# Late modulation rows summed on VectorE by half parts, partition sum by products with ones

## The chip, the cores and the metric

The kernel runs on one core of a Trainium2 chip. The metric is the device time of one execution in microseconds (us). Engines are called by the names of the profile: PE is TensorE (PEld its weight loads), DVE is VectorE, ACT is ScalarE, POOL is GpSimd, SP is SyncE, which here only issues DMAs.

## The reference, cut to what matters

One layer of a hybrid block over 1024 latent tokens and 256 context tokens, width 1024, all in fp32. The part that is changed is the modulation vector of the latent stream:

```python
mod = jax.nn.silu(c) @ w_ada[i] + b_ada[i]            # (1, 6 * 1024)
sh1, sc1, g1, sh2, sc2, g2 = jnp.split(mod[:, None, :], N_MOD, axis=-1)
...
h = modulate(rmsnorm(x, norm1_g[i]), sh1, sc1)
q, k, v, hv, hx1, hx2, gna, ghy = jnp.split(h @ w_in[i], IN_SPLITS, axis=-1)
...
x = x + g1 * gated_merge(gna, ghy, y_na, y_hy, w_na_o[i], w_hy_o[i], w_out[i])
h2 = modulate(rmsnorm(x, norm2_g[i]), sh2, sc2)
x = x + g2 * swiglu(h2, ffn_w1[i], ffn_w3[i], ffn_w2[i])
```

The parts sh1 and sc1 are needed at once. The other four (g1, sh2, sc2, g2: parts 2 to 5 of 1024 columns each) are needed only after the two mixers. For them the kernel must form, for each of 4096 columns, a sum over 1024 rows of `w_ada` times silu(c), 16 MB of weights in all.

## The kernel before, in words

The kernel runs in stages: first the early modulation and the normed, transposed input (`hidden`); then the input projection of 40 chunks of 128 columns (`project`, line 574), beside which the long convolution is done; then the attention; the gated merge; and the feed-forward part.

The projection multiplies in three products of split operands. `weights` (line 178) loads a chunk's 512 KB into the raw tile `wr` (one buffer) from SP's queue, ACT rounds it into `wh` and DVE subtracts to make `wl` (`split`, line 173), and `gemm` (line 187) issues 24 matmuls of 128x512 for each half of the tokens.

Beside it runs a generator called `side` (line 963). It first makes the spectra of the convolution's filters (`filters`, line 348, with `forward` and `dft`) merged with the late modulation rows (`ada_rows`, line 872), and then the convolutions (`conv`, line 449). `_merged` takes the next step of the generator that is least advanced by the amounts that the steps yield: 97 for the filters against 39 for `ada_rows`, and SIDE = 496 for `side` against 39 for the projection. This sets the order in which the program is written down; the framework then puts the instructions of each engine into an order of its own by readiness and by this order, and sets all waits. Each engine executes its list strictly in that order, and so does SP with the DMAs that it issues.

A filter step loads two tiles `dec` of 256 KB (two buffers), makes two products into `filt_ps` on PE and multiplies them with `dec` on DVE into `fv` (line 370). After four steps DVE does a run of sums (`fx`, `fv`, `x`, `b`, `a`: lines 378 to 430), and PE transforms the tiles `a` (`dft_ps`, lines 442 to 444) with matrices `matf`. ACT copies the results out and SP stores them (`spec`, line 390). All the products of this side work take their PSUM bank from one pool of five (`psf`).

`ada_rows` goes over two pairs of parts, (3, 4) and (2, 5). For a pair it takes a tile `arow` of 128x512, zeroes it and loads the bias into four of its rows (POOL). For each part and each k of 8 it loads 128 rows of `w_ada` over 1024 columns, 512 KB, into the ring `wal` of three, and issues four products of 256 columns, one into each group of 32 columns of the PE array (`tile_position`), with silu(c) in column 0 of the 32-column weights `cs` (line 889). They are added up in one PSUM tile `ar_ps` that is held for the whole pair. At the end one DVE addition (line 893) joins it to the bias, POOL stores the rows to DRAM, and for the first pair PE transposes them into `mod2`. Each of the 32 steps yields 1.2.

Of the kernel before, what the change touches and what calls it, by code (L numbers as in the profile page):

```python
# [10 lines left out]
F32 = mybir.dt.float32  # L11
F32R = mybir.dt.float32r
AF = mybir.ActivationFunctionType
ALU = mybir.AluOpType
# [4 lines left out]
P = 128  # L19
D = 1024  # L20
# [138 lines left out]
class Block:  # L159
# [712 lines left out]
    def ada_rows(self, pool, psf):  # L872


        nc, a = self.nc, self.a
        for pair in ((3, 4), (2, 5)):
            r = pool.tile([P, 512], F32, tag="arow", name="arow", bufs=1)
            nc.gpsimd.memset(r, 0.0)
            for n, part in enumerate(pair):
                for j in range(4):  # L880
                    at = part * D + 256 * j
                    nc.gpsimd.dma_start(r[32 * j:32 * j + 1, 256 * n:256 * n + 256], a["b_ada"][0:1, at:at + 256])
            ps = psf.tile([P, 512], F32, tag="f", name="ar_ps")
            for n, part in enumerate(pair):
                for k in range(8):
                    w = pool.tile([P, D], F32, tag="wal", name="wal", bufs=3)
                    nc.sync.dma_start(w, a["w_ada"][k, :, part * D:(part + 1) * D])
                    for j in range(4):
                        nc.tensor.matmul(ps[32 * j:32 * j + 32, 256 * n:256 * n + 256], self.cs[:, 2 * k:2 * k + 32],
                                         w[:, 256 * j:256 * j + 256], start=(k == 0), stop=(k == 7),  # L890
                                         tile_position=(0, 32 * j))
                    yield 1.2
            nc.vector.tensor_add(r, ps, r)
            for n, part in enumerate(pair):
                for j in range(4):
                    nc.gpsimd.dma_start(self.modd[part][0:1, 256 * j:256 * j + 256],
                                        r[32 * j:32 * j + 1, 256 * n:256 * n + 256])
            if pair[0] == 3:
                pt = psf.tile([P, 512], F32, tag="f", name="ada_t")
                for j in range(4):  # L900
                    nc.tensor.transpose(pt[:, j * P:(j + 1) * P], r[:, j * P:(j + 1) * P], self.ident)
                v = pt.rearrange("p (n h g q) -> p n q g h", n=2, h=2, g=4)[:, :, 0]
                cols = lambda t: t.rearrange("p (g h) -> p g h", h=2)
                nc.vector.tensor_copy(cols(self.mod2[:, 1, :]), v[:, 0])
                nc.vector.scalar_tensor_tensor(cols(self.mod2[:, 0, :]), v[:, 1], 1.0, cols(self.ng[:, 1, :]),
                                               op0=ALU.add, op1=ALU.mult)
# [207 lines left out]
    def sums(self, wa, psf, xs, raw, h2):  # L1114

        nc = self.nc
        for k in range(4):
            b = []
            for kk in (k, k + 4):
                pt = psf.tile([P, 512], F32, tag="f", name="hT_ps")  # L1120
                for j in range(4):
                    mm = nc.tensor.transpose(pt[:, j * P:(j + 1) * P], xs[j][:, kk * P:(kk + 1) * P], self.ident)
                    if j == 0:
                        self.tc.keep_in_program_order(mm)
                h = wa.tile([P, 512], F32, tag="t", name="htmp")
                nc.scalar.activation(h, pt, AF.Identity, bias=self.mod2[:, 1, kk:kk + 1],
                                     scale=self.mod2[:, 0, kk:kk + 1])
                b.append(h)
            put = lambda n, src: self.split(h2[n][0][:, k, :], h2[n][1][:, k, :], src)
            b12, b22 = b  # L1130
            b11, b21 = raw[:, k, :], raw[:, k + 4, :]
            nc.vector.tensor_sub(b11, b12, b11)
            put(5, b11)
            nc.vector.tensor_sub(b12, b22, b12)
            put(7, b12)
            nc.vector.tensor_sub(b11, b22, b11)
            put(6, b11)
            put(3, b22)
            nc.vector.tensor_sub(b21, b21, b11)
            put(4, b21)  # L1140
            yield
# [312 lines left out]
```

## Time and profile before

| | us |
|---|---|
| median of three runs | 1719.76 (1718.63 to 1722.28) |
| the profiled execution | 1721.66 |
| its span in the trace | 1719.9 |
| PE busy | 1669.8, 97% of the span |
| DVE busy | 1187.3, 69% |
| ACT busy | 662.2, 39% |

The busy time of an engine is the time in which at least one of its instructions runs; matmuls overlap in the pipeline, so that the sum of their durations is larger. An fp32 matmul appears as two instructions in the trace, so `x8` is four products. Durations are those of one profiled execution. A release ("<-") names what ended an idle time. In rows by stretch stand the stretch, its length, the busy time of PE, PEld, DVE, ACT and POOL (with their instructions), the granted PE clock as a share of full speed, the busy share of the DMA engines, and GB/s.

### The profile page before, as it was taken

To read this page: it belongs to the slowest core of one execution; us is meant where nothing else is said; L and a number is where in the kernel's file an instruction comes from. 1 tells how busy PE (TensorE), PEld (TensorE's weight loads), DVE (VectorE), ACT (ScalarE), POOL (GpSimd) and SP (SyncE) were. 2 spreads that over 40 slices of the span, in tenths; PEclk is the share of its full clock that TensorE was granted. 3 is DMA by queue.
4 is the path that set the end of the run, shared out by engine and by line. 5 is a ranking of instruction groups with operands and counts; after the bars stand their busy time and mean duration, and the time that the engine had idled before them with its cause. 6 is when DMAs were issued, how large, how long until landed. Compare 5 with 4: busy or idle time off the path is not lost.

```text
span 1719.9 us, 22909 instructions
## 1 busy us (share of the span) xinstructions
PE 1669.8 (97%) x8348; PEld 1311.0 (76%) x8348; DVE 1187.3 (69%) x2006; ACT 662.2 (39%) x1141; POOL 152.7 (9%) x273
## 2 busy tenths in 40 slices
PE   6999999999999999999999999999999999999997
PEld 2766766777777777888787788788888888878886
DVE  3665266699995966565865867867866566479566
ACT  4711222312221224455654325733333333355455
POOL 0100210101010004020200001010101001100000
PEclk9999999999999999999999999999999999999999
DMA  9375556645554456344657524333432323395344
GB/s 357 108 252 198 170 196 207 216 159 180 172 180 157 159 178 193 125 144 129 202 171 241 165 68 165 129 122 129 153 105 94 108 92 105 111 381 176 99 121 153
DMA packets 109910, 282.51 MB, mean 164 GB/s; under 512 B 15327, under 2 KB 24163, under 8 KB 107493
## 3 DMA queue, kind: packets, MB, share of 16 engines
q1 hardware_dynamic: 89864, 219.99, 38.2%
q0 software_dynamic: 19280, 60.60, 10.5%
q8 instruction: 66, 1.08, 0.3%
q10 hardware_dynamic: 653, 0.44, 0.1%
q14 instruction: 47, 0.39, 0.1%
HBM read 213.60 MB, written 67.39 MB: 163 GB/s over the span
## 4 chain that ended last, share of the span: by engine, by line
PE 44%; issue 26%; DVE 5%; DMA 5%; POOL 3%; ACT 1%; SPq 0%; POOLq 0%; ACTq 0%; DVEq 0%
PE in_ps L195 11%; PE out_ps L1091 5%; PE dx_ps L1322 5%; PE x_ps L1153 4%; PE dz_ps L1322 3%; PE dft_ps L442 2%; PE hy_ps L195 2%; PE pt_ps L800 2%; PE pt_ps L786 2%; PE na_ps L195 1%; POOL g L1266 1%; DMA ar<-g 1%; PE dft_ps L443 1%; PE dy_ps L1322 1%; PE dft_ps L444 1%
## 5 line engine op out<-in xcount | busy, mean ns | idle before, releaser
L195 PE MATMUL in_ps<-hTh,wl 128*128 128x512 f32 x640 | 259.3, 406 | 2.1 <-ACT proj L614 1.7
L195 PE MATMUL in_ps<-hTh,wh 128*128 128x512 f32 x640 | 253.2, 396 | 0.0
L195 PE MATMUL in_ps<-hTl,wh 128*128 128x512 f32 x640 | 252.6, 395 | 0.3 <-DVE hTl L176 0.2
L195 PEld LDWEIGHTS in_ps<-hTh,wl 128*128 128x128 f32 x640 | 120.7, 189 | 33.6 <-issue 5.1
L195 PEld LDWEIGHTS in_ps<-hTh,wh 128*128 128x128 f32 x640 | 120.8, 189 | 28.0 <-issue 1.6
L195 PEld LDWEIGHTS in_ps<-hTl,wh 128*128 128x128 f32 x640 | 120.9, 189 | 26.7 <-DVE hTl L176 1.9
L176 DVE TENSOR_TENSOR wl<-wr,wh 128x1024 fp32r<-128x1024 f32 (+1 forms) x56 | 59.8, 1068 | 95.7 <-ACT wh L175 95.6
L175 ACT CAST wh<-wr 128x1024 fp32r<-128x1024 f32 (+1 forms) x56 | 51.9, 926 | 135.6 <-PE in_ps L195 109.1
L176 DVE TENSOR_TENSOR ol<-ws,oh 128x512 fp32r<-128x512 f32 x88 | 60.4, 688 | 48.7 <-ACT oh L175 48.5
L176 DVE TENSOR_TENSOR ol<-ar,oh 128x512 fp32r<-128x512 f32 x77 | 52.8, 688 | 47.0 <-ACT oh L175 47.0
L175 ACT CAST oh<-ar 128x512 fp32r<-128x512 f32 x77 | 47.9, 622 | 83.6 <-PE dx_ps L1322 33.1
L175 ACT CAST oh<-ws 128x512 fp32r<-128x512 f32 x88 | 54.7, 622 | 57.5 <-PE x_ps L1153 27.4
L775 ACT ACTIVATE pe<-pe,mx 128x640 f32<-128x640 f32 x64 | 52.6, 823 | 49.3 <-DVE mx L774 49.3
L1322 PE MATMUL dx_ps<-ol,oh 128*128 128x512 f32 x176 | 68.7, 390 | 1.7 <-DVE ol L176 1.7
L442 PE MATMUL dft_ps<-a,matf 128*128 128x512 f32 x128 | 66.2, 598 | 4.0 <-DVE a L430 3.1
L1322 PE MATMUL dx_ps<-oh,ol 128*128 128x512 f32 x176 | 67.3, 390 | 2.0 <-DVE ol L176 2.0
L774 DVE CUSTOM_DVE_ANT_0 pe<-s_ps,bias 128x640 f32<-128x640 f32 x64 | 50.1, 820 | 27.7 <-PE s_ps L769 27.7
L1322 PE MATMUL dx_ps<-oh 128*128 128x512 f32 x176 | 68.5, 389 | 0.0
L175 ACT CAST oh<-wr 128x512 fp32r<-128x512 f32 x70 | 43.3, 622 | 51.5 <-PE x_ps L1153 16.0
L176 DVE TENSOR_TENSOR ol<-wr,oh 128x512 fp32r<-128x512 f32 x70 | 48.0, 688 | 21.2 <-ACT oh L175 21.0
L370 DVE TENSOR_TENSOR fv<-filt_ps,dec 128x512 f32<-128x512 f32 x32 | 21.5, 688 | 51.7 <-DMA dec<-in_decay 32.1
L1093 DVE TENSOR_TENSOR x<-x,out_ps 128x512 f32<-128x512 f32 x64 | 42.7, 684 | 19.1 <-PE out_ps L1091 18.9
(391 smaller groups left out, 4191.4 us busy)
## 6 DMA issues: line engine op xcount, KB each, us to landing
wr<-in_w SPq DMA_DIRECT2D x52, 512.0 KB, 3.6
wr<-in_w_in SPq DMA_DIRECT2D x40, 512.0 KB, 4.5
ar<-g SPq DMA_DIRECT2D x77, 256.0 KB, 2.8
wal<-in_w_ada SPq DMA_DIRECT2D x32, 512.0 KB, 6.6
matf<-in_dft_f SPq DMA_DIRECT2D x32, 384.0 KB, 4.4
bias<-in_rpb SPq DMA_DIRECT2D x64, 192.0 KB, 3.7
g<-t POOLq DMA_DIRECT2D x47, 256.0 KB, 3.0
w<-in_w SPq DMA_DIRECT2D x44, 256.0 KB, 5.4
```

What stands on the lines that cost most here:

```text
L175: self.nc.scalar.copy(hi, src)
L176: self.nc.vector.tensor_sub(lo, src, hi.bitcast(F32))
L195: mm = nc.tensor.matmul(ps, ww[:, k * P:(k + 1) * P], xx[:, k, pos:pos + width], start=(i == 0), stop=(i == n - 1))
L442: nc.tensor.matmul(ps, m[:, 0], v.rearrange("p a b -> p (a b)"), start=True, stop=False)
L774: nc.vector.tensor_tensor_reduce(pe, ps[:, 256:896], bt, -1.0, 3e38, ALU.add, ALU.min, mx[:, 0:1])
L775: nc.scalar.activation(pe, pe, AF.Exp, bias=mx[:, 0:1], scale=-1.0, accum_out=mx[:, 1:2])
L786: pin(nc.tensor.transpose(pt[:, at:at + P], pe[:, c * P:(c + 1) * P], self.ident))
L800: pin(nc.tensor.matmul(pt[ch, 1280:1408], vv[:, ch], pts[:, hh, c * P:(c + 1) * P], start=(c == 0), stop=(c == 4), tile_position=(0, 64 * ...
L1091: nc.tensor.matmul(ps, gg[x][:, tk], ww[y][:, sl], start=(i == 0), stop=(i == n - 1))
L1093: nc.vector.tensor_add(x1[:, sl], x1[:, sl], ps)
L1153: mm = nc.tensor.matmul(ps, w[u][:, k * P:(k + 1) * P], x[v][:, k, :], start=(start and k == 0 and i == 0), stop=(stop and k == 3 and i == 2),
L1322: nc.tensor.matmul(ps[j], x[u][:, j * P:(j + 1) * P], w[v], start=(start and i == 0 and c == 0), stop=(stop and i == N - 1 and k == len(re ...
```

## The change: what it does, and the diff

The products with `cs` go. Instead DVE sums over k: for each part of a pair and each half of 512 columns, eight loads of 128x512 (256 KB, ring `wal` of four, tag `wal2`) are multiplied with the column of silu(c) of their k, which is a scalar for each partition, and added into a tile `acc` (ring `aacc` of two); the first is a multiplication alone. When all eight are in, two products with a 128x32 tile of ones sum `acc` over its partitions, each over 256 columns and into a column group of its own (0 and 32 for the first half, 64 and 96 for the second), into a PSUM tile that is taken for that alone. A DVE addition of 64x256 joins it to the bias in `arow`. Each of the 64 steps yields 0.6. The bias loads, the stores and the transposition stay.

```diff
     def ada_rows(self, pool, psf):
         nc, a = self.nc, self.a
+        ones = pool.tile([P, 32], F32, name="ones", tag="ones", bufs=1)
+        nc.gpsimd.memset(ones, 1.0)
+
+        def sums(r, pair):
+            for n, part in enumerate(pair):
+                for h in range(2):
+                    acc = pool.tile([P, 512], F32, tag="aacc", name="aacc", bufs=2)
+                    for k in range(8):
+                        w = pool.tile([P, 512], F32, tag="wal2", name="wal", bufs=4)
+                        at = part * D + 512 * h
+                        nc.sync.dma_start(w, a["w_ada"][k, :, at:at + 512])
+                        c = self.cs[:, 2 * k:2 * k + 1]
+                        if k:
+                            nc.vector.scalar_tensor_tensor(acc, w, c, acc, op0=ALU.mult, op1=ALU.add)
+                        else:
+                            nc.vector.tensor_scalar(acc, w, c, None, op0=ALU.mult)
+                        yield 0.6
+                    ps = psf.tile([P, 512], F32, tag="f", name="ar_ps")
+                    for j in range(2):
+                        g = 64 * h + 32 * j
+                        nc.tensor.matmul(ps[g:g + 32, 0:256], ones, acc[:, 256 * j:256 * j + 256], start=True,
+                                         stop=True, tile_position=(0, g))
+                    rs = r[64 * h:64 * h + 64, 256 * n:256 * n + 256]
+                    nc.vector.tensor_add(rs, ps[64 * h:64 * h + 64, 0:256], rs)
+
         for pair in ((3, 4), (2, 5)):
...
-            ps = psf.tile([P, 512], F32, tag="f", name="ar_ps")
-            for n, part in enumerate(pair):
-                for k in range(8):
-                    w = pool.tile([P, D], F32, tag="wal", name="wal", bufs=3)
-                    nc.sync.dma_start(w, a["w_ada"][k, :, part * D:(part + 1) * D])
-                    for j in range(4):
-                        nc.tensor.matmul(ps[32 * j:32 * j + 32, 256 * n:256 * n + 256], self.cs[:, 2 * k:2 * k + 32],
-                                         w[:, 256 * j:256 * j + 256], start=(k == 0), stop=(k == 7),
-                                         tile_position=(0, 32 * j))
-                    yield 1.2
-            nc.vector.tensor_add(r, ps, r)
+            yield from sums(r, pair)
```

## Rows read from the trace of the kernel before

**Rows 1.** The page, part 1: engine busy us (share) x instructions.

```profile
span 1719.9 us, 22909 instructions
PE 1669.8 (97%) x8348; PEld 1311.0 (76%) x8348; DVE 1187.3 (69%) x2006; ACT 662.2 (39%) x1141; POOL 152.7 (9%) x273
```

**Rows 2.** Busy time by stage: the filters, then the convolutions.

```profile
77.00:322.00 245.00, 233.52 (x1267) 170.21 (x1267) 134.28 (x184) 52.36 (x86) 31.30 (x55) 0.98 0.61 204
322.00:640.00 318.00, 317.61 (x1337) 241.42 (x1335) 268.42 (x462) 73.88 (x107) 22.11 (x33) 1.00 0.51 173
```

**Rows 3.** The chain that ended last, in order of time: start, us, what.

```profile
287.25 11.16 PE in_ps L195 x48
...
306.84 0.43 PE dft_ps L443 x2
```

**Rows 4.** Busy time by stretch of the tile `ar_ps` alone: its last line, the sum.

```profile
sum 322.00, PE 18.78 PEld 6.29 DVE 1.37; mean PE 1.44 PEld 0.48 DVE 0.11
```

**Rows 5.** Timeline of PE around one step of `ada_rows`, and around three in a row.

```profile
97.09 0.40 PE L195 MATMUL in_ps<-hTh,wl 128*128 128x512 f32 x1
97.42 0.64 PE L889 MATMUL ar_ps<-wal,cs 128*32 128x256 f32 x8
97.98 0.50 PE L195 MATMUL in_ps<-hTl,wh 128*128 128x512 f32 x1
...
106.27 1.50 PE L889 MATMUL ar_ps<-wal,cs 128*32 128x256 f32 x24
```

**Rows 6.** Groups of DVE instructions by line and shape: busy us, mean ns | idle before.

```profile
L430 DVE SCALAR_TENSOR_TENSOR a<-x,b 128x512 f32<-128x512 f32 x64 | 42.2, 684 | 10.0 <-PE dft_ps L444 9.8
L425 DVE SCALAR_TENSOR_TENSOR x<-b 128x256 f32<-128x256 f32 x32 | 13.3, 417 | 0.0
L504 DVE TENSOR_SCALAR e<-e 128x512 f32<-128x512 f32 x8 | 3.3, 418 | 0.1
```

**Rows 7.** What PE waited for between 77 and 330 us: total, times, longest.

```profile
PE filt_ps L363 <- DVE fv L370: 2.9, 2, 2.4
PE ar_ps L889 <- DMA wal<-in_w_ada: 2.7, 3, 1.7
PE dft_ps L442 <- DVE a L430: 2.7, 1, 2.7
```

**Rows 8.** All waits between 77 and 320 us: two of DVE's.

```profile
DVE wl L176 <- ACT wh L175: 40.5, 8, 13.5
...
DVE fv L370 <- DMA dec<-in_decay: 32.1, 15, 6.8
```

**Rows 9.** What SP's queue waited for between 60 and 330 us.

```profile
SPq L181 <- DVE wl L176: 56.9, 11, 13.8
SPq L887 <- PE ar_ps L889: 49.0, 13, 11.7
```

**Rows 10.** Busy time by stretch around a PE stop, columns as in rows 2.

```profile
142.00:144.00 2.00, 0.25 (x1) 0.25 (x2) 0.69 (x1) 0.00 (x0) 0.00 (x0) 1.00 0.84 301
144.00:146.00 2.00, 1.50 (x7) 0.92 (x7) 0.69 (x1) 0.00 (x0) 0.00 (x0) 0.75 0.42 162
146.00:148.00 2.00, 2.00 (x7) 1.16 (x5) 0.69 (x1) 0.00 (x0) 0.00 (x0) 0.50 0.82 219
148.00:150.00 2.00, 2.00 (x6) 1.60 (x5) 0.69 (x1) 0.00 (x0) 0.00 (x0) 0.50 0.82 301
150.00:152.00 2.00, 2.00 (x6) 1.52 (x5) 0.69 (x1) 0.00 (x0) 0.00 (x0) 0.54 0.44 137
```

**Rows 11.** DMA issues: KB each, median us to landing.

```profile
wal<-in_w_ada SPq DMA_DIRECT2D x32, 512.0 KB, 6.6
...
dec<-in_decay SPq DMA_DIRECT2D x32, 256.0 KB, 3.9
```

**Rows 12.** Busy time by stretch inside the convolutions, columns as in rows 2.

```profile
408.00:500.00 92.00, 92.00 (x392) 69.69 (x391) 87.68 (x149) 22.79 (x32) 9.17 (x13) 1.00 0.52 175
500.00:600.00 100.00, 99.61 (x410) 75.30 (x409) 79.63 (x139) 20.16 (x29) 3.76 (x7) 1.00 0.47 160
```

## The prediction

> **What bounds the kernel now.** I read the page's engine shares first: PE is busy 97% of 1719.9 us, DVE 69% [rows 1]. Then the busy time by stage. `ada_rows` runs inside the filter stage, 77 to 322 us: there PE is busy 233.52 of 245 us and DVE only 134.28; in the convolutions behind it PE is busy 317.61 of 318 and DVE 268.42 [rows 2]. A busy PE need not be at its peak, so third comes the chain that ended last: within this stage it runs over PE, and 48 projection matmuls take 11.16 us [rows 3], 0.2325 us each. The chain shows no wait within them, and the granted clock of the stage is 0.98 of full speed [rows 2]: PE's list is the bound here, and work taken out of it is time, as long as the list stays filled. Last come the waits: PE's waits for DVE and for loads in this stage, three kinds, are 8.3 us in all [rows 7], while DVE's own idle time there is 245 − 134.28 = 110.7 us.
>
> So the question is whether work goes from the bound engine to one with room, and what the new coupling of the two costs.
>
> **The products that go.** All instructions on `ar_ps` keep PE busy 18.78 us [rows 4]. That this is time on the path, not overlap, shows in one step: the projection matmul before it starts at 97.09, the one behind it at 97.98, and without the step it would have followed after 0.2325 us; so a single step costs 0.66 us. Three steps in a row are busy 1.50 us, thus 0.43 for each further one, and 0.23 for going in and out [rows 5]. The 32 steps lie in 22 runs, counted in the timeline: 32 × 0.43 + 22 × 0.23 = 18.8 us, the same number. With them go PE's waits for the `wal` loads, 2.7 us [rows 7].
>
> **The products that come.** Eight sums (two pairs, two parts, two halves), each closed by two products of 256 columns. No row shows two column groups. One fp32 product of 256 columns over the full array takes 0.43 us (its two instructions) [rows 3], four in four column groups took the same 0.43 [rows 5]; a pair lies between these, so it is 0.43 plus 0.23 for going in and out: 8 × 0.66 = 5.3 us. Were the two groups done one after the other it would be 8 × 1.09 = 8.7 us. I take 5.3: the four groups did overlap. The Trainium skill, "TensorE: Matmul & The Clock Gate", section "Measured speedup vs the span model", puts the span of packed products at one product plus about 4 ns for each further tile; no run here shows it for two, and by it the pair would also stay at 0.66. Net for PE: −18.8 − 2.7 + 5.3 = −16.2 us.
>
> **DVE.** Per sum one multiplication, seven multiply-adds and one addition of 64x256. A multiply-add of 128x512 lasts 684 ns, a 128x512 multiplication by a scalar 418, an operation of 256 columns 417 [rows 6]. 8 × (7 × 0.684 + 0.418 + 0.417) = 45.0 us, less the two old additions of 0.69: +43.6. DVE's load in the stage goes to 134.3 + 43.6 = 178 us of some 229, 78%. That is room on average, so I cost the work itself at nothing: its cover is the 110.7 us of idle time, most of it DVE standing at `wl` for ACT's rounding (40.5 us) and at `fv` for `dec` (32.1) [rows 8]. But DVE keeps its order. A multiply-add written behind such a wait stands with it, and the runs that end in the tiles `a`, which PE needs, get longer by the multiply-adds mixed in. In return a multiply-add that stands for its load holds up `fv`, `wl` and `a` behind it, and PE waits for all three.
>
> **The new wait.** PE's pair of products waits for the eighth multiply-add, and the projection's matmuls stand behind it in PE's list. The old steps waited for a load alone, 2.7 us over 32. The nearest rows: PE's waits for DVE at `filt_ps` and `dft_ps` were 5.6 us over 64 groups of products, at most 2.66 us each [rows 7]. Bounds for eight pairs are thus 8 × 0.09 = 0.7 us and 8 × 2.66 = 21.3 us. Nothing below zero: a wait that is added gives nothing back. I take 0.5 us a pair, 4 us, nearer the lower end, since the framework places the pair by readiness and has projection matmuls to put before it, as with `dft_ps`; but the chain is longer (eight loads, eight dependent sums), and the real landing times vary.
>
> **Loads.** The bytes stay; 32 loads of 512 KB become 64 of 256 KB. The former landed after 6.6 us, `dec` loads of 256 KB on the same queue after 3.9 [rows 11], so a half costs less than a whole. The ring holds 1 MB ahead instead of 1.5. SP's order matters more: it stood 49.0 us because PE had not released a `wal` buffer, and `dec`, `matf`, `spec` and `wr` stood behind; 56.9 us it stood at `wr` [rows 9]. DVE will release the halves instead. I take zero here, with −2 (earlier `dec`) and +3 us (DVE in its long waits releases late) as bounds, about PE's whole wait for `fv` today [rows 7] to either side. 32 more issues are hidden by SP's idle time.
>
> **PSUM, POOL, clock.** `ar_ps` no longer holds one of five banks for a whole pair; a small gain within the −2. POOL gets one small memset. After PE had stopped around 142 us (0.25 us busy in 2) its clock was granted at 0.50, that is 1.2 GHz, for some six us, which by the shares 0.75, 0.50, 0.50 and 0.54 lost 3.4 us [rows 10]. That dip may vanish or another come: 3.4 to either side.
>
> **Sum.** −18.8 − 2.7 + 5.3 + 4 = −12.2 us. Against the profiled execution, 1721.66, this is 1709.5; the median of the runs lies 1.9 us below that execution, so I expect 1707.6, say 1708. Bounds: with waits at 0.7, loads −2 and the dip gone 1719.76 − 16.2 + 0.7 − 2 − 3.4 = 1699; with serial pairs (+3.4), loads +3 and another dip 1707.6 + 9.8 = 1717.
>
> **Rivals.**
>
> *DVE's chain sets the end of the stage.* Then PE's 13.5 us return as idle time. For it: between 408 and 500 us DVE is busy 87.68 of 92 us, so filters that end no earlier can't be caught up there. Against: between 500 and 600 it has 20 us of room [rows 12], and today's long DVE waits are for PE's progress (`wl` behind ACT behind the projection) and shrink with it. Only the load waits come back: 1719.76 − 2.7 = 1717. The Trainium skill, "Trainium Kernel Development and Optimization", section "Performance Expectations", speaks for this rival: it calls matmul busy time a bad measure of the distance to the peak, so PE at 97% might not be the bound. The trace disagrees for this stage: 48 matmuls follow one another every 0.2325 us with no wait in the chain [rows 3].
>
> *The pairs stop PE.* Place: the pair behind the eighth multiply-add. Price: 2.66 us each, the longest that PE has waited for DVE here [rows 7], 8 × 2.66 = 21.3 us; net −16.2 + 21.3 = +5.1, so 1725, and 3.4 more for each stop that lowers the clock. It decides from 16.2 / 8 = 2.0 us a pair. For it: DVE stands up to 13.5 us in one wait [rows 8], and a multiply-add behind it can be late by as much. Against: the two waits of 2.4 and 2.7 us are the only long ones for DVE in some 64 groups of products.
>
> *More comes back than I count.* Freed SP queue and bank end PE's waits for `fv` (2.9) and `a` (2.7) and the dip: 1719.76 − 16.2 + 0.7 − 5.6 = 1699, about 1700 with the dip left as it is.
>
> **How the numbers follow.** Chances: the forecast 0.52, DVE's chain 0.17, stopped pairs 0.21, the larger gain 0.10. About 0.2%, 3.4 us, is what a measurement of this kernel can tell from no change: 1716.3 to 1723.2. Faster: 0.52 + 0.10 + 0.02 of DVE's chain = 0.64; the rest of that rival is "the same", 0.15; slower 0.21. The range goes from 1699 to 1724: below it I leave some 0.05, above it the worse part of the stopped pairs, about 0.13.
>
> **What would show it.** In the profile after: `ar_ps` products about 5 us of PE (8 pairs, 32 instructions); multiply-adds of 684 ns, 56 of them; DVE 178 us busy in a filter stage that is some 12 us shorter, PE there as full as before, and the convolutions of the same length. PE's wait at `ar_ps` for `aacc` about 4 us. Wrong it would be if that wait passes 16 us, if PE's idle time in the stage grows by as much as its work shrinks, if `dft_ps` or `in_ps` wait longer for `a` or `wl`, or if the granted clock falls in more places.

## The result, and the profile after

The changed kernel takes 1712.44 us (median of six runs, 1710.85 to 1714.26) against 1722.20 for the kernel before (median of six): ratio 0.9943, 95% interval 0.9927 to 0.9960. That is 9.8 us faster; the forecast was 11.8, and the range 1699 to 1724 holds the time. The forecast stood on 1719.76 us for the kernel before, the median of its first three runs; against that the changed kernel is 7.3 us faster. The profiled execution took 1714.26, its span is 1712.2 against 1719.9 us. One execution of all that follow was slow (1849.27 us at a granted clock of 0.847, in the run with thin multiply-adds), and the ratios leave it out.

The page of the changed kernel, part 1, as in [rows 1]:

```profile
span 1712.2 us, 22620 instructions
...
PE 1655.7 (97%) x8124; PEld 1305.4 (76%) x8124; DVE 1230.1 (72%) x2076; ACT 662.3 (39%) x1141; POOL 153.8 (9%) x274
```

PE lost 14.1 us of work, but the span only 7.7: PE's idle time grew from 50.1 to 56.5 us. Where the span changes, one tile shows: the convolutions' first and last load of `u`, before and after (the kernel before first; the numbers behind the durations are the first and the last start):

```profile
L454 SPq DMA_DIRECT2D u<-z x4: 320/326/327, 330.5 to 560.1; - x4
...
L454 SPq DMA_DIRECT2D u<-z x4: 320/326/327, 323.0 to 552.6; - x4
```

Both came 7.5 us earlier, and the end 7.7. So what follows the filter stage is neither helped nor hurt, and nearly all of the gain lies in the stage: some 0.8 us of it stands already ahead of the new instructions (the store of `qk` starts at 67.22 us before and at 66.45 after) and can be the scatter of single executions. The stage itself, from 77 us to the same point before the end as in [rows 2]:

```profile
77.00:314.30 237.30, 219.97 (x1040) 164.85 (x1040) 177.30 (x255) 52.96 (x86) 31.24 (x54) 0.97 0.64 211
```

PE is busy 13.5 us less than in [rows 2] and idle 17.3 us instead of 11.5; DVE is busy 177.30 us, which was 134.28. The new groups of DVE and the two kinds of loads, as in [rows 6] and [rows 11]:

```profile
L890 DVE SCALAR_TENSOR_TENSOR aacc<-wal,cs,aacc 128x512 f32<-128x512 f32 x56 | 41.8, 746 | 25.7 <-DMA wal<-in_w_ada 25.1
L892 DVE TENSOR_SCALAR aacc<-wal,cs 128x512 f32<-128x512 f32 x8 | 3.8, 480 | 0.7 <-DMA wal<-in_w_ada 0.6
L900 DVE TENSOR_TENSOR arow<-ar_ps,arow 64x256 f32<-64x256 f32 x8 | 3.3, 418 | 0.1
```

```profile
wal<-in_w_ada SPq DMA_DIRECT2D x64, 256.0 KB, 4.4
...
dec<-in_decay SPq DMA_DIRECT2D x32, 256.0 KB, 3.1
```

PE around one pair of products with ones, as in [rows 5], and the group of all of them:

```profile
291.96 0.62 PE L897 MATMUL ar_ps<-aacc,ones 128*32 128x256 f32 x4
292.52 0.50 PE L195 MATMUL in_ps<-hTh,wl 128*128 128x512 f32 x1
```

```profile
L897 PE MATMUL ar_ps<-aacc,ones 128*32 128x256 f32 x32 | 5.0, 390 | 1.4 <-issue 1.4
```

A pair keeps PE 0.62 us, a group of four kept it 0.64. No view names a wait of the products for `aacc`, but PE stood once ahead of a pair:

```profile
PE ar_ps L897 <- issue: 1.4, 1, 1.4
```

"issue" means that the profile names no releaser. The pair starts at 106.65 us, and the last multiply-add of its sum ran on DVE until 106.44, so the wait was very likely for this one. What PE waited for in the stage instead, as in [rows 7], and three of DVE's waits, as in [rows 8]:

```profile
PE filt_ps L363 <- DVE fv L370: 9.5, 4, 3.8
PE dft_ps L442 <- DVE a L430: 3.2, 3, 2.0
```

```profile
DVE aacc L890 <- DMA wal<-in_w_ada: 25.1, 15, 4.7
...
DVE fv L370 <- DMA dec<-in_decay: 18.3, 10, 3.6
...
DVE wl L176 <- ACT wh L175: 11.4, 5, 4.1
```

PE's wait for `fv` rose from 2.9 to 9.5 us. Most of it is two stops, of 3.85 and 3.75 us. DVE's wait for `dec` fell from 32.1 [rows 8] to 18.3 us, so how long DVE stands does not by itself tell how long PE does. The second stop, seen on DVE, then PE, then SP:

```profile
255.01 2.32 DVE L890 SCALAR_TENSOR_TENSOR aacc<-wal,cs,aacc 128x512 f32<-128x512 f32 x3
261.67 0.75 DVE L890 SCALAR_TENSOR_TENSOR aacc<-wal,cs,aacc 128x512 f32<-128x512 f32 x1 [4.34 <-DMA wal<-in_w_ada]
262.45 1.29 DVE L370 TENSOR_TENSOR fv<-filt_ps,dec 128x512 f32<-128x512 f32 x2
```

```profile
263.20 2.07 PE L363 MATMUL filt_ps<-fw,hid 64*128 64x256 f32 x6 [3.75 <-DVE fv L370]
```

```profile
256.24 0.44 SPq L887 DMA_DIRECT2D wal<-in_w_ada  x1
```

A half part is issued at 256.24 and used at 261.67; DVE stands at it for 4.34 us, `fv` is written behind it, and PE stands for `fv`. At the other stop, at 140 us, DVE stood at `fv` itself, for a `dec` whose load SP had issued at 133.94 with three loads of the sums right behind it:

```profile
139.32 1.29 DVE L370 TENSOR_TENSOR fv<-filt_ps,dec 128x512 f32<-128x512 f32 x2 [3.15 <-DMA dec<-in_decay]
```

```profile
140.06 2.07 PE L363 MATMUL filt_ps<-fw,hid 64*128 64x256 f32 x6 [3.85 <-DVE fv L370]
```

The clock fell at both; the two ten-microsecond stretches with the stops (columns as in [rows 2], the clock third from the end):

```profile
137.00:147.00 10.00, 6.94 (x20) 5.11 (x21) 5.17 (x8) 0.00 (x0) 0.00 (x0) 0.66 0.82 269
...
257.00:267.00 10.00, 5.93 (x26) 3.90 (x23) 4.42 (x8) 0.58 (x1) 0.00 (x0) 0.73 0.82 296
```

### The profile page after: what moved, and what is told of

It reads as the page before. It is cut to its first block, busy times and chain, and to the rows that moved or that the text cites. A ratio compares the mean times of both kernels' runs of the same rounds, so it can differ in the third digit from the quotient of the medians.

```text
span 1712.2 us, 22620 instructions
## 1 busy us (share of the span) xinstructions
PE 1655.7 (97%) x8124; PEld 1305.4 (76%) x8124; DVE 1230.1 (72%) x2076; ACT 662.3 (39%) x1141; POOL 153.8 (9%) x274
## 4 chain that ended last, share of the span: by engine, by line
PE 66%; issue 8%; DVE 4%; DMA 3%; ACT 1%; POOL 0%; SPq 0%; DVEq 0%; POOLq 0%; ACTq 0%
PE x_ps L1169 15%; PE in_ps L195 13%; PE z_ps L1169 7%; PE dx_ps L1338 5%; PE out_ps L1107 5%; PE dz_ps L1338 3%; PE dft_ps L442 2%; PE hy_ps L195 2%; PE y_ps L1169 2%; PE pt_ps L800 2%; PE pt_ps L786 2%; PE dft_ps L443 1%; PE dft_ps L444 1%; PE dy_ps L1338 1%; PE s_ps L766 1%
## 5 line engine op out<-in xcount | busy, mean ns | idle before, releaser
L774 DVE CUSTOM_DVE_ANT_0 pe<-s_ps,bias 128x640 f32<-128x640 f32 x64 | 50.1, 820 | 28.1 <-PE s_ps L769 28.1
L175 ACT CAST oh<-wr 128x512 fp32r<-128x512 f32 x70 | 43.3, 622 | 52.7 <-PE x_ps L1169 17.3
L890 DVE SCALAR_TENSOR_TENSOR aacc<-wal,cs,aacc 128x512 f32<-128x512 f32 x56 | 41.8, 746 | 25.7 <-DMA wal<-in_w_ada 25.1
L1109 DVE TENSOR_TENSOR x<-x,out_ps 128x512 f32<-128x512 f32 x64 | 42.7, 684 | 18.6 <-PE out_ps L1107 18.3
```

The costliest lines, as they stand in the source:

```text
L175: self.nc.scalar.copy(hi, src)
L774: nc.vector.tensor_tensor_reduce(pe, ps[:, 256:896], bt, -1.0, 3e38, ALU.add, ALU.min, mx[:, 0:1])
L890: nc.vector.scalar_tensor_tensor(acc, w, c, acc, op0=ALU.mult, op1=ALU.add)
L1109: nc.vector.tensor_add(x1[:, sl], x1[:, sl], ps)
```

## The experiments

The question is what made the new idle time. Theory A: the loads of the sums, either because DVE stands at them or because `dec` comes late beside them. Theory B: the added DVE work. All ratios are to the kernel before, with 95% intervals; the kernel before took 1719.4 to 1721.0 us in these rounds. A profile is one execution and may lie some us off its median; the verdicts rest on the ratios. Every edit also gives each engine another order, and one run below changes the order alone: it moved the ratio by 0.0033, some 6 us. So a smaller difference between two runs need not come from what was edited.

**No loads.**

```diff
+        w = pool.tile([P, 512], F32, tag="wal2", name="wal", bufs=1)
+        nc.sync.dma_start(w, a["w_ada"][0, :, 2 * D:2 * D + 512])
...
-                        w = pool.tile([P, 512], F32, tag="wal2", name="wal", bufs=4)
-                        at = part * D + 512 * h
-                        nc.sync.dma_start(w, a["w_ada"][k, :, at:at + 512])
```

> The changed kernel, but one 128x512 block of w_ada is loaded once and used for all 64 multiply-adds: 63 of the 64 loads of the sums are left out, all work on DVE and PE stays. Theory A (the part of the gain that is missing was lost because DVE stands at a multiply-add for its load, 25 us in 15 waits, or at fv for a dec that shares the DMA engines with these loads, so that PE stops at filt_ps, 9.5 us against 2.9 before): PE's wait for fv falls below 3 us, no stop of over 2 us, and the time is some 8 us below the changed kernel's, about 1704. Theory B (the 47 us of added DVE work delay fv and a, whatever the loads do): waits and time stay, 1711 to 1713.

Measured: 1701.04 us, 0.9883 (0.9867 to 0.9898). Its stage and PE's wait:

```profile
77.00:297.20 220.20, 212.30 (x1030) 161.46 (x1030) 176.11 (x251) 50.48 (x83) 30.41 (x52) 0.99 0.47 152
```

```profile
PE filt_ps L363 <- DVE fv L370: 4.2, 3, 2.5
```

With DVE as busy as in the changed kernel (176 us), the time is 10 us lower, and PE's idle time in the stage is 7.9 us, below that of the kernel before. PE's busy time in the stage fell too, by 7.7 us, though PE has the same instructions in the whole kernel; some 3.7 of these are the clock, which fell once instead of twice (an estimate: busy time times what the granted clock lacked of full speed, summed by single microseconds, 1.7 us here and 5.4 in the changed kernel). This profile is of the fastest execution, 3 us below the median. The wait did not quite fall below 3 us, and one stop of 2.5 stayed. The time speaks for theory A, by more than the run with another order alone moved it, and against theory B's 1711 to 1713.

**Thin multiply-adds.**

```diff
-                            nc.vector.scalar_tensor_tensor(acc, w, c, acc, op0=ALU.mult, op1=ALU.add)
+                            nc.vector.scalar_tensor_tensor(acc[:, 0:32], w[:, 0:32], c, acc[:, 0:32], op0=ALU.mult,
+                                                           op1=ALU.add)
```

> The changed kernel, but the multiply-adds cover 32 of their 512 columns: the sums are left out for the other columns, the loads, their order and their ring stay. DVE loses about 56 x 0.6 = 34 us of work. Theory A (standing for loads): PE's stops at filt_ps stay, about 9 us, and the time is 1711 to 1713. Theory B (the work itself): the stops go and the time falls by 6 to 8 us, to about 1705.

Measured: 1709.72 us (median of five), 0.9932 (0.9916 to 0.9948), an interval that overlaps that of the changed kernel for most of its width. PE and DVE wait much as there:

```profile
PE filt_ps L363 <- DVE fv L370: 7.0, 4, 2.3
```

```profile
DVE aacc L890 <- DMA wal<-in_w_ada: 33.6, 24, 5.0
```

DVE was relieved of 26 us of busy time (177.30 to 150.85 in the stage), and it stood 8.5 us longer for the loads. The 6 to 8 us of theory B did not come; 2 us, within the uncertainty, did. Theory B gets no support from this side either.

**No sums at all.** All lines of `sums` but its two outer loops are taken out; one yield of 4.8 stands for the eight of 0.6.

> The changed kernel without the sums at all: loads, multiply-adds, products with ones and their additions are left out, the bias rows alone go on. What is left of the price of the late modulation shows as the difference. If the prediction's terms hold (5.0 us of products on PE) and the stops at filt_ps are the sums' doing (6.6 us more than before, and one more fall of the clock, about 3 us), the time is 12 to 15 us below the changed kernel's, 1697 to 1700. If the stops belong to the filters themselves (dec loads), only the 5 us of products go: about 1707.

Measured: 1703.22 us, 0.9898 (0.9881 to 0.9915). Neither branch of the expectation: between 1700 and 1707. With neither loads nor DVE work, PE still waits for `fv`. The stage, PE's wait and DVE's:

```profile
77.00:303.50 226.50, 211.10 (x999) 162.31 (x998) 130.06 (x177) 51.50 (x84) 31.40 (x55) 0.97 0.44 143
```

```profile
PE filt_ps L363 <- DVE fv L370: 9.5, 3, 5.1
```

```profile
DVE fv L370 <- DMA dec<-in_decay: 32.0, 13, 4.9
```

So the stops are not the sums' alone: the filters make them too, when `dec` comes late (PE's longest stop here, 5.15 us, ends right after DVE had stood 4.91 us for `dec`), and where they fall depends on the order that the framework finds. The 9.5 us are as many as in the changed kernel. This run lies 9.2 us below the changed kernel; 5.0 of these are the pairs, so that some 4 us are left for the loads and the DVE work together, where the run without loads gave 10 for the loads alone.

The run without loads, which does all DVE work and all products of the sums, is not slower than this one (0.9883 against 0.9898, the intervals overlap). The 47 us of DVE work are hidden to within what can be measured. The eight pairs are not hidden, they keep PE busy for 5.0 us; there PE's idle time in the stage is smaller, 7.9 us against 15.4.

**Another order.**

```diff
-                        yield from _merged((fgen, 97), (self.ada_rows(fp, psf), 39))
+                        ada, got, due = self.ada_rows(fp, psf), 0, 0
+                        for n in fgen:
+                            n = 1 if n is None else n
+                            yield n
+                            if n > 1.5:
+                                due += n * 39 / 76.8
+                                while got < due:
+                                    m = next(ada, None)
+                                    got += 100 if m is None else m
+                                    if m is not None:
+                                        yield m
+                        yield from ada
```

> The changed kernel with another order alone: the steps of the sums are written only beside the filter steps that run on DVE and PE (the run of sums and the transforms), none beside the steps that load dec and make fv. All work is done. Theory A: dec no longer shares the DMA engines with the loads of the sums and DVE does not stand at a multiply-add ahead of fv, so PE's wait for fv falls below 4 us and the time by 4 to 7 us, to about 1706. Theory B: DVE's runs towards the tiles a get longer, PE's wait for a grows by as much, and the time stays or rises, 1712 to 1716.

Measured: 1716.98 us, 0.9976 (0.9963 to 0.9989), slower than the changed kernel. PE's wait for `fv` stayed at 9.2 us in 6 stops, the longest 4.1, and that for `a` was one stop of 3.7. Writing the steps elsewhere in the program did not take the waits away: DVE still stood 24.1 us at `aacc` and 19.0 at `fv`. As a test of theory A it is inconclusive; as a remedy it failed. What it does show is the price of an order: all work is the same, and 0.9943 became 0.9976.

**Loads that nobody reads**, in three forms, to part DVE's standing from the traffic: as the run without loads, with one buffer for `acc`, and in each step

```diff
+                        x = pool.tile([P, 512], F32, tag="wal2", name="wal", bufs=4)
+                        at = part * D + 512 * h
+                        nc.sync.dma_start(x, a["w_ada"][k, :, at:at + 512])
```

> As in the run without loads, DVE's multiply-adds all read one block that is loaded once, so the sums are not those of the reference; but now all 64 loads of 256 KB are issued as well, into the ring of four, and nobody reads them. DVE stands at no load of the sums, while the DMA engines and SP's queue carry them all (the tile acc has one buffer here, for room). If the loss is DVE standing at a multiply-add ahead of fv, the time stays at that of the run without loads, about 1701. If it is the DMA engines, shared with the loads dec, or SP's queue, the time returns to that of the changed kernel, about 1712, with PE's wait for fv at 7 us or more.

then with `x[:, 0:64]` and 64 columns in the load:

> As the run with loads that nobody reads, but each of the 64 loads brings 128x64 elements, 32 KB, an eighth of the bytes; number, queue, ring and DVE's work are the same, and the sums are not those of the reference. If the bytes on the DMA engines make dec and matf late, the time is that of the run without loads, 1700 to 1703. If it is the 64 issues in SP's order and their completions, it is that of the full loads that nobody reads, 1709 to 1714.

then with full loads from `nc.gpsimd`:

> As the run with 64 full loads that nobody reads, but issued from POOL's queue: the bytes on the DMA engines stay, SP's order is free of them, and DVE stands at none. If the loads' place in SP's order is what costs, the time is that of the run without loads, 1700 to 1704. If the bytes cost, it stays at 1709 to 1714. The small loads that nobody reads gave 1708 in between, so a result in between would say that both do.

Measured: 1713.10 us, 0.9953 (0.9937 to 0.9969) for full loads on SP's queue; 1708.12 us, 0.9930 (0.9906 to 0.9954) for small ones; 1722.11 us, 1.0001 (0.9983 to 1.0019) for full ones on POOL's queue. The first says that the loss comes back although DVE stands at no load of the sums: 0.9883 to 0.9953, some 12 us. DVE's standing, seen in the stop at 263 us, is one form of it, not the cause of all. SP's order is not out of the question here, since SP stood 28.4 us, in 31 waits, for the load before in the same buffer, with the loads of `dec` behind. The one buffer for `acc` is not what costs (its control, below, gave 0.9931 with everything else as in the changed kernel). The profile of this kernel fell on its fastest execution, span 1706.4 us, and does not show the wait for `fv` of 7 us that was expected; PE's waits there are spread:

```profile
PE dft_ps L442 <- issue: 3.2, 2, 2.3
PE filt_ps L363 <- DVE fv L370: 3.2, 3, 1.6
PE dft_ps L442 <- DMA matf<-in_dft_f: 2.8, 1, 2.8
```

The third speaks against SP's order as the only cause: there SP is free of these loads, and DVE stood longer for `dec` than in any other run:

```profile
DVE fv L370 <- DMA dec<-in_decay: 34.4, 14, 7.4
```

```profile
PE filt_ps L363 <- DVE fv L370: 11.1, 3, 8.6
```

But that run adds something of its own: PE stood 7.7 us at `dft_ps` for nothing that the profile names, 5.3 of them in one stop. The second, between its two branches, does not fit the bytes as sole cause: with an eighth of them 0.9930 remains, and its interval overlaps that of the full loads. What of the loads costs, bytes or number, is not settled by these runs. Each of them also has an order of its own on every engine.

**Loads of the sums on POOL's queue**, all work done (`nc.gpsimd.dma_start` in place of `nc.sync.dma_start`).

> The changed kernel with the loads of the sums issued from POOL's queue instead of SP's. All work done. If SP's order is what makes loads late (it stands at a wal load for DVE, 33 us, with dec, matf and wr behind), these waits go and the time falls to 1704 to 1708. If the DMA engines' bandwidth is the limit, no change: 1710 to 1714. POOL has its own stores (z, vtok, qk) in order; if they are held behind the loads, ACT's and the convolutions' start gets later and the time rises.

Measured: 1733.15 us, 1.0075 (1.0058 to 1.0091). Neither 1704 to 1708 nor no change but the third branch, a rise: it costs 21 us against the changed kernel. That POOL's own stores were held up, as that branch has it, is not shown: ahead of the stores of `z` POOL stood 47.3 us for ACT. POOL stands for DVE to release the ring, PE for `fv`:

```profile
POOL wal L887 <- DVE aacc L890: 47.5, 39, 3.7
POOL wal L887 <- DVE aacc L892: 21.4, 3, 11.4
```

```profile
PE filt_ps L363 <- DVE fv L370: 12.8, 5, 6.6
```

**More room for `dec`.** The last link of the stop at 140 us, and of the longest one in the run with no sums, is a late `dec`, whose ring is two deep. With three buffers, and one for `acc` instead of two:

```diff
-                        dec.append(pool.tile([P, 512], F32, tag="dec", name="dec", bufs=2))
+                        dec.append(pool.tile([P, 512], F32, tag="dec", name="dec", bufs=3))
...
-                    acc = pool.tile([P, 512], F32, tag="aacc", name="aacc", bufs=2)
+                    acc = pool.tile([P, 512], F32, tag="aacc", name="aacc", bufs=1)
```

> The changed kernel, all work done, with three buffers for dec instead of two, and one for acc instead of two to make room. If PE's long stops come from dec being loaded too late (its load is issued only when fv has read the one two before), they go: wait for fv below 4 us, time 1704 to 1707. If they come from DVE standing at the loads of the sums, or from the DMA engines being full, the time stays within 2 us of the changed kernel's, 1710 to 1714. One buffer for acc costs a wait of the next sum's first multiplication for the products with ones, at most 8 times.

the control with the second edit alone:

> The changed kernel with one buffer for acc instead of two, nothing else: the control for the runs in which room was made that way. If the gain with three buffers for dec is dec's, this one is the changed kernel's time or a little above, 1711 to 1716. If the one buffer itself (another order of the sums) brings it, about 1704.

four buffers for `dec`, three for `wal`, one for `acc`:

> As the run with three buffers for dec, but four for dec and three for wal. If dec's lateness is the cause, at least as good as with three, 1702 to 1707. If DVE's standing at the loads of the sums is the cause, the shallower ring makes it worse than the changed kernel: 1714 to 1720.

and the kernel before with three for `dec` and two for its `wal`:

> The kernel before, with three buffers for dec and two instead of three for its loads of 512 KB; the products on PE stay. If the late dec is the filters' own weakness, this gains as well, 4 to 7 us below the kernel before (ratio about 0.997). If it hurts only where DVE does the sums, nothing is gained: ratio 0.999 to 1.004, the shallower ring may cost some.

Measured: three for `dec` 1703.96 us, 0.9905 (0.9888 to 0.9923); the control 1709.96 us, 0.9931 (0.9913 to 0.9950); four and three 1708.89 us, 0.9934 (0.9914 to 0.9953); the kernel before 1722.14 us, 1.0008 (0.9991 to 1.0026). With three for `dec`, the stage and its waits:

```profile
77.00:300.90 223.90, 214.84 (x1037) 162.61 (x1038) 173.21 (x248) 52.21 (x85) 31.03 (x53) 0.99 0.68 223
```

```profile
PE filt_ps L363 <- DVE fv L370: 2.8, 4, 1.8
```

```profile
DVE aacc L890 <- DMA wal<-in_w_ada: 9.3, 4, 4.0
DVE fv L370 <- DMA dec<-in_decay: 8.5, 8, 2.9
```

It is faster than the changed kernel, the intervals do not touch, and it is the fastest of all kernels here that do the whole work: 16 us below the kernel before. Its first branch came true, 1704 and a wait below 4 us, in a profile of its fastest execution. Against its control it is 0.0026, 4 to 5 us, and the intervals overlap by 0.001; the waits point to `dec`: 8.5 us at `fv` for `dec` against 18.3 in the control, PE's wait for `fv` 2.8 against 6.5. That the gain is `dec`'s is likely, not shown. With four for `dec` and only three for `wal`, `fv` waited 4.9 us for `dec` but `aacc` 19.3 for its loads, in a profile of its slowest execution, and most of the gain was gone (the intervals overlap). The two rings share one pool of memory; this run suggests that each needs its depth. In the kernel before the same edit brought nothing; its `wal` ring had to shrink for it (PE's wait for `wal` rose from 2.7 to 6.2 us), and its profile is of its slowest execution, so whether `dec` alone would have helped there stays open.

## Why the prediction was right or wrong, point by point

- **The bound: right, on less than it says.** The chain that the prediction reads reaches back only to 285 us within this stage. That PE was the bound in the rest of it rests on PE's idle time, 11.5 of 245 us [rows 2].
- **The products that go and come: right.** PE's busy time on `ar_ps` fell from 18.78 [rows 4] to 5.0 us; 5.3 was forecast. A pair costs what a group of four cost, as taken. The 2.7 us of waits for `wal` [rows 7] are gone. By the Trainium skill, "TensorE: Matmul & The Clock Gate", section "Measured speedup vs the span model", a pair should differ from a group of four by some 8 ns, an estimate from its figure of about 4 ns for each further tile; the trace shows 0.62 or 0.63 against 0.64 us, which agrees to within 12 ns.
- **That freed PE time is time: right, for the larger part.** Of 13.5 us of PE's work in the stage 5.8 came back as idle time; the convolutions' first load came 7.5 us earlier and the end 7.7. "DVE's chain sets the end of the stage", by which all 13.5 would have come back, did not happen. PE was not "as full as before" in the stage: 93% instead of 95%.
- **DVE's work: mis-sized, and rightly costed at nothing.** The multiply-adds lasted 746 ns, not 684, and the multiplications 480, not 418: 56 × 0.746 + 8 × 0.480 + 8 × 0.418 = 49.0, net 47.6 us where 43.6 was forecast. The rows taken [rows 6] have a constant as scalar; here it is a column of `cs`. The run with thin multiply-adds and the run without loads both show that this work is hidden.
- **The new wait: wrong in place.** 4 us were put down for PE at the products with ones; there PE stood 1.4 us, once. More went to another place, `filt_ps` for `fv`: +6.6 us. The text had named it ("a multiply-add that stands for its load holds up `fv`, `wl` and `a` behind it") but gave it no price of its own.
- **Loads at zero, −2 to +3: the step that was mis-sized.** The upper bound was put at PE's whole wait for `fv`, some 3 us; this wait rose by 6.6, more than twice that. Each of its two long stops ends at a late load, one of the sums ahead of `fv` in DVE's order, one of `dec`. How much of the rise the loads of the sums make is only bounded: from the changed kernel the run without loads lies 10 us away, the run with no sums some 4 us apart from the pairs, and that run has the same 9.5 us at `fv`. The rest can be order; no run parts the two. "A half costs less than a whole" (4.4 against 6.6 us landing) was right, and SP did stand less at these loads (43.5 us in all its waits for them, 52.3 before, of which 49.0 stand in [rows 9]); neither kept PE's wait from rising.
- **The clock: 3.4 us to either side; it moved nothing.** The stop of [rows 10] was not the only fall before: between 77 and 87 us the clock was lower too (columns as in [rows 2]). So the stage had two falls before and two after, and what they took from PE is, by the estimate above, 5.1 and 5.4 us. The sign "if the granted clock falls in more places" did not come.

```profile
77.00:87.00 10.00, 8.59 (x55) 6.73 (x54) 3.86 (x5) 2.64 (x4) 5.02 (x10) 0.83 0.86 288
```

- **The rival of stopped pairs** did not happen as told: one pair of eight waited, 1.35 us. In the run with four buffers for `dec` and three for `wal` one waited 3.4 us for its multiply-add. But the rival's mechanism, a PE stop for DVE in order, occurred at `fv`, at 3.85 and 3.75 us, longer than the 2.66 us that bounded it. **The larger gain** was not reached, but the kernel with three buffers for `dec` reached 1704. The sum of that rival names the end of the dip and does not take off its 3.4 us; with them it would be 1695.

The sum: PE's work −13.5, its idle time +5.8, gives −7.7 us for the spans of the profiled executions where −12.2 was forecast; the medians differ by 9.8. That the time came so near is in part luck: PE's terms, the largest, were right, but the 4 us given to one wait stood in for a wait elsewhere, which has another cause.

## What to carry to other kernels

When work is moved from the bound engine to one with idle time, price the loads that the new engine will wait for, not only its instructions: in an engine that keeps its order, each wait for a load is a wait of everything written behind it. The arithmetic that moved was free here to within what the runs can tell; leaving out its loads gave 10 us. Part of such a difference can be the new order: here another order alone moved the time by some 6 us. Look then for the neighbour whose ring is shallowest: one more buffer for `dec`, with one less for `acc`, brought some 6 us (0.9943 to 0.9905), of which 4 to 5 stand against the control with the one buffer less alone, and that buffer was not missed (0.9931).

## What the runs showed of the hardware that was not expected

- A DVE multiply-add of 128x512 whose scalar is a column in memory lasts 746 ns, with a constant 684 [rows 6]; a multiplication by a column 480, by a constant 418 [rows 6]. It is 62 ns either way.
- With 64 loads of 256 KB that nobody reads the kernel took some 12 us longer than without them (0.9883 to 0.9953), and some 20 us longer with the same loads from POOL's queue (1.0001). How they cost is open: traffic, SP's order and the new order of the engines are not parted.
- The two PE stops of 3.8 us in the changed kernel were each followed by a lower granted clock: 0.66 and 0.73 in the mean of the ten microseconds around them.
